# A hybrid attention block: two gates ahead in the merge queue, a first norm that carries its gain, and mask additions and zero fills on VectorE

## The chip, the cores and the metric

The kernel runs on one core of a Trainium2 chip. TensorE (PE) multiplies, VectorE (DVE) and ScalarE (ACT) do element-wise work, GpSimd (POOL) a few additions and subtractions, and the queue of SyncE (SP) issues nearly all DMAs. The metric is device time of the whole program in microseconds (us). A difference is called none when it stays within 1% of the time before.

## The reference

One layer on a sequence of 512 tokens and 1024 model columns, all in float32:

```python
h = _rms(x, norm1_g)                       # x * rsqrt(mean(x*x) + eps) * g
(a_q, a_k, a_v, i_q, i_k, i_w, b_q, b_kv, b_g, c_qkv, mix_g) = _split_last(h @ w_in, IN_SIZES)
y_a = _dsa_attention(...) @ w_branch_a     # 8 heads, keys chosen by an indexer's top 128
y_b = _nsa_attention(...) @ w_branch_b     # 8 heads: compressed, selected-block and window parts
y_c = _dilated_attention(...) @ w_branch_c # 12 heads at strides 1, 4 and 16, mixed by their sums
g = jax.nn.sigmoid(mix_g)                  # 3 x 1024 gate columns
x = x + (g_A * y_a + g_B * y_b + g_C * y_c) @ w_out
h = _rms(x, norm2_g)
gate, up = jnp.split(h @ w_ffn_in, 2, axis=-1)
x = x + (jax.nn.silu(gate) * up) @ w_ffn_out
```

In branch A the selection is an additive mask: the bias table of a head plus, per query and key, zero or a large negative number (`topm`). The softmax adds that sum to the logits.

## The kernel before, in words

**Matrix products.** Every large product is made of three matmuls on halves of the numbers: each operand is a rounded part (`hi`) and a remainder (`lo`), and `mm3` (L106 to L108) adds hi·hi, hi·lo and lo·hi. `weights` (L89 to L102) loads pieces of a weight matrix (`raw`, issued by SP), ScalarE rounds them to `whi` (L81) and VectorE, for some pieces GpSimd, subtracts to `wlo` (L82).

**First norm.** `norm_sums` squares a token tile (128 tokens) in two halves, one on ScalarE (L162), one on VectorE (L164). `norm_T` multiplies by the reciprocal root (halves on VectorE L176 and ScalarE L178), transposes on TensorE into the PSUM pool `tr` of two buffers (L111), multiplies by the gain column `gT` (L188, tile `gx`), and splits into `xh` and `xl`, the latter on GpSimd for one half and VectorE for the other. `gT` is loaded as 1024 single elements.

**Order of the work.** The program is written as a stream of projections and gates, with the attention branches as generators: each `tick` advances every started generator by one step. A scheduler turns this into a fixed order on each engine, so an instruction that is not ready stops all behind it on its engine. DMAs share eight completion lanes: a ninth waits until the lane of the first is free, in the order of issue.

**Gates and merges.** Of each branch (in the order B, A, C) and each of 8 column groups, `gate` (L949) computes the gate with 24 matmuls of 128x512 and two ticks, and `merge` (L965) multiplies the branch's output by its weights (12 matmuls, for C 6) and adds it to the sum in DRAM (`dz`). The list `due` holds gates whose merge is still to come; `ready` ticks the attention on, with nothing between, until the branch's output is there. In the trace a gate matmul reads `pm<-xh` or `pm<-xl`, a merge matmul `pm<-oT`.

**Softmax of a head's query tile** (L538 to L565): logits `lg` on TensorE, table added and maximum on VectorE (L547), exponent on ScalarE (L562), division on VectorE (L563, L564), then transposes of `p`. For branch A with a mask, GpSimd first makes `tabm` = table + `topm` (L557), 24 times.

**Branch C.** `c_load` (L755) brings back projected queries and keys (`c_in`, 12 DMAs, five buffers that it shares with `p`); `c_prep` transposes them one after the other, loads values (`c_v`) and, by 24 small DMAs for two heads, the bias tables (`ctab`, L246). GpSimd zero-fills four buffers `pt12` (L831), of which the last 128 columns of each half are later written whole.

Of the kernel before, what the change touches and what calls it, by code (L numbers as in the profile page):

```python
# [11 lines left out]
F32 = mybir.dt.float32  # L12
# [3 lines left out]
ALU = mybir.AluOpType  # L16
# [51 lines left out]
def block_kernel(ctx: ExitStack, tc: tile.TileContext, x, norm1_g, norm2_g, w_in, qk_norm_g, cmp_pos, cmp_w,  # L68
# [58 lines left out]
    xts = []  # L127
    ipx = ExitStack()
    ip = ipx.enter_context(tc.tile_pool(name="init", bufs=1))
    with tc.high_priority():  # L130
        for t in range(NT):
            xt = ip.tile([128, D], F32, name=f"x{t}")
            nc.sync.dma_start(xt, x[t * 128:(t + 1) * 128, :])
            xts.append(xt)
    gT = ip.tile([128, KC], F32, name="gT")
    nc.scalar.dma_start(gT, norm1_g[0].rearrange("(k p) -> p k", p=128))
    ident = cp.tile([128, 128], F32, name="ident")
    make_identity(nc, ident)
    mhalf = cp.tile([128, 16], F32, name="mhalf")
# [27 lines left out]
    def norm_T(xt, t, ss, n, g, xh, xl, pst, tmp, lo):  # L167

        s1 = ty.tile([128, 16], F32, name="nss", tag="ss")
        nc.vector.tensor_reduce(out=s1[:, 0:1], in_=ss[:, 0:n], op=ALU.add, axis=AX.X)  # L170
        r = rstd(s1, 1, 1.0 / D)
        hn = tmp.tile([128, D], F32, name="hn", tag="hn", bufs=2)
        for q in range(2):
            hs = slice(q * 512, q * 512 + 512)
            if q == 0:
                nc.vector.tensor_scalar(out=hn[:, hs], in0=xt[:, hs], scalar1=r[:, 0:1], scalar2=None, op0=ALU.mult)  # L176
            else:
                nc.scalar.activation(hn[:, hs], xt[:, hs], AF.Copy, scale=r[:, 0:1])  # L178
        yield
        for q in range(2):  # L180
            ps = pst()
            for k in range(4):
                transpose(ps[:, k, :], hn[:, (4 * q + k) * 128:(4 * q + k + 1) * 128])
            ts = slice(t * 128, (t + 1) * 128)
            if g is not None:
                g3 = g[:, 4 * q:4 * q + 4].unsqueeze(2).to_broadcast([128, 4, 128])
                gx = tmp.tile([128, 4, 128], F32, name="gx", tag="gx", bufs=2)
                nc.vector.tensor_tensor(out=gx, in0=ps, in1=g3, op=ALU.mult)  # L188
                ps = gx
            split(xh[:, 4 * q:4 * q + 4, ts], xl[:, 4 * q:4 * q + 4, ts], ps, eng=lo[q])  # L190

    ps1 = ExitStack()
# [13 lines left out]

    xh = xp.tile([128, KC, S], F32R, name="xh", tag="xh")
    xl = xp.tile([128, KC, S], F32R, name="xl", tag="xl")
    for t in range(NT):
        ss = ty.tile([128, 16], F32, name="nss", tag="ss")  # L210
        norm_sums(ss, xts[t], ip)
        for _ in norm_T(xts[t], t, ss, 2, gT, xh, xl, tr_tile, ip, (nc.gpsimd, nc.vector)):
            pass
    nc.sync.dma_start(mk, masks)
    for hh in range(2):
# [33 lines left out]
        return bass.AP(tensor=tab.tensor, offset=tab.offset + hi - 1, ap=[list(tab.ap[0]), [-1, hi - lo]])  # L249


    def proj_tm(segs, evac, then=None):
        width = sum(n for _, n in segs)
        wk = weights(w_in, segs, list(range(KC)), pool=PP)
        for t in range(NT):
            ps = mm_tile()
            ts = slice(t * 128, (t + 1) * 128)
            mm3(ps[:, 0:width], [((xh[:, k, ts], xl[:, k, ts]), wk[k]) for k in range(KC)])
            evac(t, ps)
            tick()  # L260
        if then is not None:
            start(then())
# [19 lines left out]
            yield  # L282

    def tmt(name):
        return ap_.tile([128, NT, 256], F32, name=name, tag="tm", bufs=3)

    def norm_heads(tm, c0, nh):

# [77 lines left out]
    def narrow():  # L366
        aik = scratch4k([128, NT, 256], "aik")

        def evac(t, ps):
            for j, c in enumerate((0, 128)):  # L370
                nc.scalar.copy(undup(aik[:, t, 128 * j:128 * j + 128], 1), dup(ps[:, c:c + 64], 1))
            nc.vector.tensor_copy(av[:, t, :], ps[:, 64:128])
            nc.vector.tensor_copy(iw[:, t, :], ps[:, 192:196])
            nc.scalar.activation(bgt[:, t, :], ps[:, 196:220], AF.Tanh, scale=0.5)  # L374

        def then():
            nc.vector.tensor_scalar(out=bgt, in0=bgt, scalar1=1.0, scalar2=0.5, op0=ALU.add, op1=ALU.mult)
            nc.vector.tensor_scalar(out=bg4[:, 0, :, 0], in0=bg4[:, 0, :, 0], scalar1=live, scalar2=None, op0=ALU.mult)
            norm_heads(aik, 0, 2)
            yield from wait(0)  # L380
            st_["ik"] = k_stack(aik, 128, None)
            yield
            while len(st_.get("iq", ())) < 4:
                yield
            for i in range(1, NT):
                yield from scores(i)
            st_["ak"] = k_stack(aik, 0, gain[:, 1:2])
            yield
            for i in range(1, NT):
                yield from select(i)  # L390

        proj_tm([(C_AKV, 128), (C_IK, 68), (C_BG, 24)], evac, then=then)

    def scores(i):
        w = 128 * (i + 1)
# [154 lines left out]
    def causal_probs(q, i, k, tab, topk, gate):  # L550
        w = 128 * (i + 1)
        lg = lg_tile()
        last_qk[0] = qk(lg[:, 0:w], q, i, k)
        tab = rev(tab, 0, w)
        if topk is not None:
            tm_ = ab.tile([128, S], F32, name="tabm", tag="tabm", bufs=2)
            nc.gpsimd.tensor_tensor(out=tm_[:, 0:w], in0=tab, in1=topk, op=ALU.add)  # L557
            tab = tm_[:, 0:w]
        p = ap_.tile([128, S], F32, name="p", tag="p", bufs=5)
        m = ty.tile([128, 4], F32, name="m", tag="m")  # L560
        add_table(p[:, 0:w], lg[:, 0:w], tab, 3e38, m[:, 0:1])
        nc.scalar.activation(p[:, 0:w], p[:, 0:w], AF.Exp, bias=m[:, 0:1], scale=-1.0, accum_out=m[:, 1:2])  # L562
        nc.vector.reciprocal(m[:, 2:3], m[:, 1:2])  # L563
        nc.vector.tensor_scalar(out=p[:, 0:w], in0=p[:, 0:w], scalar1=m[:, 2:3], scalar2=gate, op0=ALU.mult,  # L564
                                op1=ALU.bypass if gate is None else ALU.mult)  # L565
        return p
# [225 lines left out]
    def c_prep(hf, cz, ld):  # L792
        for g in range(3):
            for s in "qk":
                if hf == 1:
                    c_load()
                    yield
                t_ = c_in.pop((hf, g, s))
                ps = tr_cols(t_, 0)
                if g == 0:  # L800
                    ld[s, g] = (near_queries if s == "q" else near_keys)(hf, cz, ps)
                    if len(c_jobs) > 6:
                        c_load()
                    yield
                    continue
                cq = cz.tile([128, S], F32, name="cq", tag="cq", bufs=8)
                dst = cq
                if s == "q":
                    dst, ps = cq.rearrange("p (i r w) -> p i r w", i=NT, r=4), ps.rearrange("p (i w r) -> p i r w", i=NT, r=4)
                elif g:  # L810
                    dst, ps = cq.rearrange("p (r u) -> p r u", r=4), ps.rearrange("p (u r) -> p r u", r=4)
                nc.scalar.activation(dst, ps, AF.Copy, scale=(gain8[:, 4:5] if s == "q" else gain[:, 5:6]))
                ld[s, g] = cq
                if len(c_jobs) > 6:
                    c_load()
                yield
            rows = dV[g, :, 128 * hf:128 * hf + 128]
            v_ = cz.tile([128, NT, 128], F32, name="c_v", tag="cv", bufs=6)
            nc.sync.dma_start(v_, rows.rearrange("(u r) c -> u r c", r=NT) if g else
                              rows.rearrange("(t p) c -> p t c", p=128))  # L820
            ld["v", g] = v_
        for j in range(2):
            h = 2 * hf + j
            tab = cz.tile([128, S], F32, name="ctab", tag="ctab", bufs=4)
            for r in range(4):
                rows = tab[32 * r:32 * r + 32]
                vec_table(rows[:, 0:256], 16 + h, V_C0 + r, [[4, 32], [1, 256]])
                vec_table(rows[:, 256:384], 20 + h, V_C1, [[1, 32], [1, 128]])
                vec_table(rows[:, 384:512], 24 + h, V_C2, [[1, 32], [1, 128]])
            pt = cz.tile([128, 2, NT, 128], F32, name="pt12", tag="pt12", bufs=3)  # L830
            nc.gpsimd.memset(pt, 0.0)  # L831
            ld["tab", j], ld["pt", j] = tab, pt

    def c_unit(hf, i, j, ld, d):
# [116 lines left out]
    def gate(bi, f):  # L951
# [6 lines left out]
        for k0 in range(0, KC, 4):  # L958
            mm3(pg, [((wg[k][0][:, cs], wg[k][1][:, cs]), (xh[:, k, :], xl[:, k, :])) for k in range(k0, k0 + 4)], k0, KC)
            tick()  # L960
        tz = ap_.tile([128, 2, S], F32, name="tz", tag="tm", bufs=3)
        nc.scalar.activation(tz[:, 0, :], pg, AF.Tanh, scale=0.5)
        return tz

# [62 lines left out]
    for bi in (1, 0, 2):  # L1027
        for f in range(KC):
            due.append((bi, f, gate(bi, f)))
            if len(due) > 1:  # L1030
                if due[0][1] == 0:
                    ready(due[0][0])
                merge(*due.pop(0))
# [137 lines left out]
```

## Time and profile before

| | us |
|---|---|
| median of 3 runs | 993.58 (992.93 to 999.28) |
| the profiled execution, own time | 991.78 |
| its span | 990.0 |
| PE / DVE / ACT / POOL busy | 971.0 / 564.9 / 436.5 / 174.0 |

How to read it: busy time is the sum of an engine's instructions, and matmuls overlap one another a little, so TensorE's 98% does not say that it never waits. The chain of waits follows the last instruction back to what released it, step by step. In a timeline row the idle time in brackets is what the engine waited just before, with the releaser; a row may hold several like instructions.

### The profile page before, as it was taken

The numbers are of one execution on the slowest core, as the hardware profiler recorded it, in microseconds if no ns is written. First come the engines' busy times: TensorE is split into PE (matmuls) and PEld (weight loads), VectorE is DVE, ScalarE is ACT, GpSimd is POOL, SyncE is SP. The second block draws the span as 40 slices with busy tenths as digits, with TensorE's granted clock in tenths as the row PEclk, the third lists the DMA queues.
The fourth block names the chain that finished last, engine by engine and source line by source line (L and its number), as shares of the span: only waits on it lengthen the run. The fifth ranks groups of instructions, "written<-read, shape, count | busy, mean of one in ns | idle before, by whom it ended". The sixth has DMA issues, their size and how long they took to land.

```text
span 990.0 us, 16079 instructions
## 1 busy us (share of the span) xinstructions
PE 971.0 (98%) x5887; PEld 823.7 (83%) x5887; DVE 564.9 (57%) x1277; ACT 436.5 (44%) x956; POOL 174.0 (18%) x156
## 2 busy tenths in 40 slices
PE   6999999999999899999999999999999999999998
PEld 5889999899887577777778899988888888888886
DVE  6699999766665666574764645454344344422321
ACT  5544555756565655564534434443333233322220
POOL 3234565543100221131110312000000000000000
PEclk9999999999999999999999999999999999999999
DMA  8541344433332244367613452233333333322421
GB/s 210 123 128 44 86 119 128 120 116 110 104 96 66 79 129 121 118 167 195 187 57 89 140 201 86 86 101 110 88 88 108 104 85 96 110 93 96 139 75 42
DMA packets 119264, 109.91 MB, mean 111 GB/s; under 512 B 19931, under 2 KB 105234, under 8 KB 119186
## 3 DMA queue, kind: packets, MB, share of 16 engines
q1 hardware_dynamic: 116994, 107.85, 37.6%
q10 hardware_dynamic: 2192, 1.05, 0.4%
q8 instruction: 46, 0.75, 0.3%
q14 instruction: 32, 0.26, 0.1%
HBM read 96.66 MB, written 12.21 MB: 110 GB/s over the span
## 4 chain that ended last, share of the span: by engine, by line
PE 93%; DMA 3%; DVE 2%; ACT 1%; issue 1%; SPq 1%; POOL 0%; DVEq 0%; ACTq 0%; POOLq 0%
PE pf L107 14%; PE pf L108 14%; PE pf L106 14%; PE pm L107 13%; PE pm L106 13%; PE pm L108 13%; PE tr L111 4%; PE ovb L541 2%; PE lg L364 2%; PE lg L363 2%; PE ova L541 1%; DMA c_in<-dC 1%; PE lg L849 1%; DMA raw<-in_w_in 1%; DMA raw<-in_w_branch_a 1%
## 5 line engine op out<-in xcount | busy, mean ns | idle before, releaser
L82 DVE TENSOR_TENSOR wlo<-raw,whi 128x512 fp32r<-128x512 f32 (+1 forms) x243 | 182.4, 756 | 146.1 <-ACT whi L81 145.1
L81 ACT CAST whi<-raw 128x512 fp32r<-128x512 f32 (+1 forms) x288 | 176.9, 619 | 175.0 <-PE pf L108 80.8
L107 PE MATMUL pm<-wlo,xh 128*128 128x256 f32 (+1 forms) x512 | 145.5, 287 | 0.3 <-DVE wlo L82 0.3
L106 PE MATMUL pm<-whi,xh 128*128 128x256 f32 (+1 forms) x512 | 145.1, 288 | 0.6 <-ACT bgt L374 0.6
L108 PE MATMUL pm<-whi,xl 128*128 128x256 f32 (+1 forms) x512 | 144.8, 285 | 0.5 <-POOL xl L82 0.5
L107 PE MATMUL pf<-xl,whi 128*128 128x512 f32 (+1 forms) x384 | 142.6, 372 | 0.1
L106 PE MATMUL pf<-xh,whi 128*128 128x512 f32 (+1 forms) x384 | 142.5, 372 | 0.0
L108 PE MATMUL pf<-xh,wlo 128*128 128x512 f32 (+1 forms) x384 | 142.0, 371 | 0.0
L107 PEld LDWEIGHTS pm<-wlo,xh 128*128 128x128 f32 x512 | 98.1, 192 | 1.9 <-issue 0.8
L108 PEld LDWEIGHTS pm<-whi,xl 128*128 128x128 f32 x512 | 98.2, 192 | 1.4 <-POOL xl L82 0.8
L106 PEld LDWEIGHTS pm<-whi,xh 128*128 128x128 f32 x512 | 97.7, 193 | 1.2 <-ACT bgt L374 0.8
L108 PE MATMUL pm<-xh,wlo 128*128 128x512 f32 x224 | 88.8, 396 | 0.0
L106 PE MATMUL pm<-xh,whi 128*128 128x512 f32 x224 | 88.7, 396 | 0.0
L107 PE MATMUL pm<-xl,whi 128*128 128x512 f32 x224 | 88.1, 393 | 0.0
L107 PEld LDWEIGHTS pf<-xl,whi 128*128 128x128 f32 x384 | 72.3, 188 | 12.5 <-DVE xl L82 0.3
L106 PEld LDWEIGHTS pf<-xh,whi 128*128 128x128 f32 x384 | 72.2, 188 | 12.5
L108 PEld LDWEIGHTS pf<-xh,wlo 128*128 128x128 f32 x384 | 72.2, 188 | 12.6
L82 POOL TENSOR_TENSOR wlo<-raw,whi 128x512 fp32r<-128x512 f32 x45 | 62.2, 1404 | 111.6 <-ACT whi L81 100.8
L106 PE MATMUL pf<-whi,hh 128*128 128x512 f32 x176 | 69.4, 395 | 0.0
L108 PE MATMUL pf<-whi,hl 128*128 128x512 f32 x176 | 69.4, 395 | 0.0
L107 PE MATMUL pf<-wlo,hh 128*128 128x512 f32 x176 | 69.4, 395 | 0.0
L562 ACT ACTIVATE p<-p,m 128x128 f32<-128x128 f32 (+3 forms) x96 | 53.8, 561 | 27.2 <-DVE m L547 26.0
(312 smaller groups left out, 1691.0 us busy)
## 6 DMA issues: line engine op xcount, KB each, us to landing
raw<-in_w_in SPq DMA_DIRECT2D x92, 256.0 KB, 3.1
raw<-in_w_ffn_in SPq DMA_DIRECT2D x88, 256.0 KB, 2.9
raw<-in_w_ffn_out SPq DMA_DIRECT2D x44, 256.0 KB, 2.8
raw<-in_w_in SPq DMA_DIRECT2D x52, 128.0 KB, 2.6
x<-in_x SPq DMA_DIRECT2D x8, 512.0 KB, 6.0
tab<-dvec SPq DMA_DIRECT2D x16, 256.0 KB, 3.3
dz<-tz SPq DMA_DIRECT2D x16, 256.0 KB, 2.5
tz<-dz SPq DMA_DIRECT2D x16, 256.0 KB, 3.3
```

What stands on the lines that cost most here:

```text
L81: nc.scalar.copy(dst_hi, src)
L82: (eng or nc.vector).tensor_tensor(out=dst_lo, in0=src, in1=dst_hi.bitcast(F32), op=ALU.subtract)
L106: nc.tensor.matmul(ps, ah, bh, start=(j == 0), stop=False)
L107: nc.tensor.matmul(ps, ah, bl, start=False, stop=False)
L108: nc.tensor.matmul(ps, al, bh, start=False, stop=(j == n - 1))
L111: nc.tensor.transpose(dst, src, ident[0:src.shape[0], 0:src.shape[0]])
L363: nc.tensor.matmul(lg, qs, k[:, 0, 0:w], start=True, stop=False)
L364: return nc.tensor.matmul(lg, qs, k[:, 1, 0:w], start=False, stop=stop)
L541: mm = nc.tensor.matmul(ov[64 * j:64 * j + 64, 128 * b:S], v(b), pts[j][:, 4 * b:3 * b + NT, :], start=first and b == 0, stop=last and b = ...
L562: nc.scalar.activation(p[:, 0:w], p[:, 0:w], AF.Exp, bias=m[:, 0:1], scale=-1.0, accum_out=m[:, 1:2])
L849: nc.tensor.matmul(lg[32 * r:32 * r + 32, c:c + n], ld["q", g][hp, 128 * i + 32 * r:128 * i + 32 * r + 32], ld["k", g][hp, 128 * r:128 * r ...
```

## The change

The gain row `g_row` (one DMA of 1024 contiguous elements) is spread over the partitions by two matmuls with a row of ones, into two PSUM tiles. `norm_T` multiplies by root and gain in one VectorE instruction, before the transposes; the multiplication after them is gone, `xh` and `xl` are made from the transposes' PSUM tile, and VectorE makes all of `xl`. Squares are taken by ScalarE alone. The first weights are loaded from an earlier place in the text (SP's order of the first loads comes out as before). VectorE makes `tabm`, in the buffers `work`, and zero-fills `pt12` without the columns that are written later. `due` holds one gate more, with a fourth buffer.

```diff
+    NARROW = [(C_AKV, 128), (C_IK, 68), (C_BG, 24)]
+    g_row = ip.tile([1, D], F32, name="g_row")
+    nc.scalar.dma_start(g_row, norm1_g[0:1, :])
+    one = ip.tile([1, 128], F32, name="one")
+    nc.vector.memset(one, 1.0)
...
-    gT = ip.tile([128, KC], F32, name="gT")
-    nc.scalar.dma_start(gT, norm1_g[0].rearrange("(k p) -> p k", p=128))
+            if t == 1:
+                w_narrow = weights(w_in, NARROW, list(range(KC)))
...
-        nc.vector.tensor_reduce(out=s1[:, 0:1], in_=ss[:, 0:n], op=ALU.add, axis=AX.X)
-        r = rstd(s1, 1, 1.0 / D)
+        if n > 1:
+            nc.vector.tensor_reduce(out=s1[:, 0:1], in_=ss[:, 0:n], op=ALU.add, axis=AX.X)
+        r = rstd(s1 if n > 1 else ss, 1, 1.0 / D)
...
-            if q == 0:
+            if g is not None:
+                nc.vector.scalar_tensor_tensor(out=hn[:, hs], in0=xt[:, hs], scalar=r[:, 0:1], in1=g[q], op0=ALU.mult,
+                                               op1=ALU.mult)
+            elif q == 0:
...
-            if g is not None:
-                g3 = g[:, 4 * q:4 * q + 4].unsqueeze(2).to_broadcast([128, 4, 128])
-                gx = tmp.tile([128, 4, 128], F32, name="gx", tag="gx", bufs=2)
-                nc.vector.tensor_tensor(out=gx, in0=ps, in1=g3, op=ALU.mult)
-                ps = gx
...
+    gps = [lg_tile() for _ in range(2)]
+    for q in range(2):
+        nc.tensor.matmul(gps[q], one, g_row[:, 512 * q:512 * q + 512], start=True, stop=True)
...
-        norm_sums(ss, xts[t], ip)
-        for _ in norm_T(xts[t], t, ss, 2, gT, xh, xl, tr_tile, ip, (nc.gpsimd, nc.vector)):
+        norm_sums(ss, xts[t], ip, n=1)
+        for _ in norm_T(xts[t], t, ss, 1, gps, xh, xl, tr_tile, ip, (nc.vector, nc.vector)):
...
-        return ap_.tile([128, NT, 256], F32, name=name, tag="tm", bufs=3)
+        return ap_.tile([128, NT, 256], F32, name=name, tag="tm", bufs=4)
...
-            tm_ = ab.tile([128, S], F32, name="tabm", tag="tabm", bufs=2)
-            nc.gpsimd.tensor_tensor(out=tm_[:, 0:w], in0=tab, in1=topk, op=ALU.add)
+            tm_ = ab.tile([128, S], F32, name="tabm", tag="work", bufs=3)
+            nc.vector.tensor_tensor(out=tm_[:, 0:w], in0=tab, in1=topk, op=ALU.add)
...
-            nc.gpsimd.memset(pt, 0.0)
+            nc.vector.memset(pt[:, :, 0:NT - 1, :], 0.0)
...
-        tz = ap_.tile([128, 2, S], F32, name="tz", tag="tm", bufs=3)
+        tz = ap_.tile([128, 2, S], F32, name="tz", tag="tm", bufs=4)
...
-            if len(due) > 1:
+            if len(due) > 2:
```

The first place is VectorE's order where branch B has ended and branch A's softmaxes begin again. Before:

```order
L564 TENSOR_SCALAR p<-p,m 128x256
L582 TENSOR_TENSOR oT<-ovb,oT 128x512
L563 RECIPROCAL m<-m 128x1
L547 ISA p,m<-lg,tabm 128x512
L547 ISA m 128x1
L563 RECIPROCAL m<-m 128x1
L564 TENSOR_SCALAR p<-p,m 128x384
```

In the change:

```order
L589 TENSOR_TENSOR oT<-ovb,oT 128x512
L571 TENSOR_SCALAR p<-p,m 128x256
L564 TENSOR_TENSOR tabm<-tab,topm_1580 128x256
L571 TENSOR_SCALAR p<-p,m 128x384
L564 TENSOR_TENSOR tabm<-tab,topm_1580 128x256
L554 ISA p,m<-lg,tabm 128x512
```

Two additions of 256 columns now stand among the divisions that the transposes wait for; one of 384 and two of 512 stand up to 16 rows ahead of them.

The second place is SP's order where branch C's inputs are loaded, from the first `c_in` to the tables. Before:

```order
L93 DMA raw<-in_w_branch_a 128x2x256 x2
L761 DMA c_in<-dC 128x4x128 x2
L93 DMA raw<-in_w_in 128x2x256
L761 DMA c_in<-dC 128x4x128 x2
L93 DMA raw<-in_w_in 128x2x256
L761 DMA c_in<-dC 128x4x128 x2
L819 DMA c_v<-dV 128x4x128 x3
L246 DMA ctab<-dvec 32x256
```

In the change:

```order
L93 DMA raw<-in_w_branch_a 128x2x256
L93 DMA raw<-in_w_in 128x2x256 x4
L768 DMA c_in<-dC 128x4x128 x6
L826 DMA c_v<-dV 128x4x128 x3
L253 DMA ctab<-dvec 32x256
```

Behind these stand, in both, the rest of the 24 `ctab` DMAs and only then the seventh `c_in`. One store of `dz` stands among the tables in both, one `raw` before and two in the change.

The third place is TensorE's order at the sixth and seventh of the `c_in` transposes. Before:

```order
L106 MATMUL pm<-xh,whi 128x512
L107 MATMUL pm<-xl,whi 128x512
L108 MATMUL pm<-xh,wlo 128x512
L111 MATMUL tr<-ident,c_in 128x128 x4
L849 MATMUL lg<-cq 32x32 x8
L106 MATMUL pm<-xh,whi 128x512
L107 MATMUL pm<-xl,whi 128x512
L108 MATMUL pm<-xh,wlo 128x512
L106 MATMUL pm<-xh,whi 128x512
L107 MATMUL pm<-xl,whi 128x512
L111 MATMUL tr<-ident,c_in 128x128 x4
```

In the change:

```order
L106 MATMUL pm<-oT,whi 128x512
L107 MATMUL pm<-oT,whi 128x512
L111 MATMUL tr<-ident,c_in 128x128 x4
L856 MATMUL lg<-cq 32x32 x4
L111 MATMUL tr<-ident,c_in 128x128 x4
L856 MATMUL lg<-cq 32x32 x4
L108 MATMUL pm<-oT,wlo 128x512
```

The seventh transposes have moved up: from the first `c_in` transposes to the seventh there were 32 gate and 30 merge matmuls, and now there are 24 and 20, while the rest between them stays but for four small `lg<-cq`.

## Rows read from the trace of the kernel before

**Rows 1.** The page: busy time per engine; the chain's shares by engine
```profile
PE 971.0 (98%) x5887; PEld 823.7 (83%) x5887; DVE 564.9 (57%) x1277; ACT 436.5 (44%) x956; POOL 174.0 (18%) x156
PE 93%; DMA 3%; DVE 2%; ACT 1%; issue 1%; SPq 1%; POOL 0%; DVEq 0%; ACTq 0%; POOLq 0%
```

**Rows 2.** Windows: length, busy and instructions of PE, PEld, DVE, ACT, POOL, clock, DMA
```profile
350.00:430.00 80.00, 80.00 (x415) 63.74 (x415) 48.85 (x127) 43.48 (x106) 19.32 (x19) 1.00 0.37 109
540.00:990.00 450.00, 446.24 (x2242) 379.29 (x2240) 186.45 (x293) 143.15 (x257) 22.33 (x26) 1.00 0.34 103
```

**Rows 3.** SP's waits from 0 to 30 us: total, times, longest
```profile
SPq L93 <- DMA gT<-in_norm_g: 1.3, 1, 1.3
```

**Rows 4.** PE's timeline, start: start, length, instruction, idle before and releaser
```profile
13.07 0.55 PE L108 MATMUL pm<-whi,xl 128*128 128x220 f32 x1 [0.49 <-POOL xl L82]
18.14 0.53 PE L107 MATMUL pm<-wlo,xh 128*128 128x220 f32 x1
18.67 0.27 PE L106 MATMUL pm<-whi,xh 128*128 128x220 f32 x1
```

**Rows 5.** Groups from 0 to 35 us: busy, mean ns, idle before
```profile
L82 POOL TENSOR_TENSOR xl<-gx,xh 128x512 fp32r<-128x512 f32 x4 | 5.4, 1356 | 6.7 <-ACT xh L81 6.6
L188 DVE TENSOR_TENSOR gx<-tr,gT 128x512 f32<-128x512 f32 x8 | 5.4, 683 | 0.1
L82 DVE TENSOR_TENSOR xl<-gx,xh 128x512 fp32r<-128x512 f32 x4 | 3.7, 922 | 1.7 <-ACT xh L81 1.7
```

**Rows 6.** Line 238, a float32 matmul with few rows: shortest, median, longest ns
```profile
L238 PE MATMUL lg<-oh,rel x6: 536/546/557, 49.6 to 68.5; 33*28 33x448 f32 x6
```

**Rows 7.** PE's timeline where only the attention runs
```profile
328.56 0.55 PE L111 MATMUL tr<-ident,p 128*128 128x128 f32 x3 [0.73 <-ACT pT L530]
330.02 0.66 PE L111 MATMUL tr<-ident,p 128*128 128x128 f32 x4 [0.42 <-ACT pT L530]
331.36 0.65 PE L111 MATMUL tr<-ident,p 128*128 128x128 f32 x4 [0.68 <-DVE qst L321]
332.71 4.02 PE L541 MATMUL ovb<-pT,bv 128*64 128x512 f32 x16 [0.52 <-ACT pT L530]
```

**Rows 8.** DVE's groups from 320 to 435 us
```profile
L564 DVE TENSOR_SCALAR p<-p,m 128x256 f32<-128x256 f32 x8 | 5.6, 705 | 0.2
L547 DVE CUSTOM_DVE_ANT_0 p<-lg,tabm 128x512 f32<-128x512 f32 x8 | 5.5, 684 | 4.0 <-PE lg L364 4.0
L547 DVE CUSTOM_DVE_ANT_0 p<-lg,tabm 128x384 f32<-128x384 f32 x8 | 4.4, 552 | 2.2 <-PE lg L364 2.1
L547 DVE CUSTOM_DVE_ANT_0 p<-lg,tabm 128x256 f32<-128x256 f32 x8 | 3.4, 423 | 8.3 <-PE lg L364 8.3
L564 DVE TENSOR_SCALAR p<-p,m,bgt 128x256 f32<-128x256 f32 x2 | 0.8, 410 | 0.0
```

**Rows 9.** DVE's timeline at the end of branch A
```profile
432.00 0.48 DVE L564 TENSOR_SCALAR p<-p,m 128x512 f32<-128x512 f32 x1
437.76 0.69 DVE L582 TENSOR_TENSOR oT<-ova,oT 128x512 fp32r<-128x512 f32 x1 [4.61 <-ACT oT L581]
```

**Rows 10.** PE's timeline, from branch A's last logits to branch C's preparation
```profile
429.22 0.39 PE L363 MATMUL lg<-kst,qst 128*128 128x512 f32 x1
434.16 0.63 PE L111 MATMUL tr<-ident,c_in 128*128 128x128 f32 x4
434.72 2.38 PE L541 MATMUL ova<-pT,av 128*64 128x512 f32 x16
443.44 0.40 PE L108 MATMUL pm<-xh,wlo 128*128 128x512 f32 x1
446.64 0.40 PE L107 MATMUL pm<-xl,whi 128*128 128x512 f32 x1
456.61 0.63 PE L111 MATMUL tr<-ident,c_in 128*128 128x128 f32 x4 [0.95 <-DMA c_in<-dC]
```

**Rows 11.** SP's timeline there: start and length of the DMA issues
```profile
434.07 1.89 SPq L761 DMA_DIRECT2D c_in<-dC  x2
436.01 2.97 SPq L819 DMA_DIRECT2D c_v<-dV  x3
445.44 6.96 SPq L246 DMA_DIRECT2D ctab<-dvec  x15
452.50 0.52 SPq L761 DMA_DIRECT2D c_in<-dC  x1
```

**Rows 12.** The DMAs of `c_in`, issue to landing: shortest, median, longest us
```profile
DMA to landing us min/median/max: 3.5/4.0/4.3
```

**Rows 13.** The chain of waits at the eighth `c_in`: start, length, what
```profile
462.86 3.66 DMA c_in<-dC
```

More of the change, by code (lines that the diff above doesn't have):

```diff
@@ L249, in rev, with proj_tm @@
         return bass.AP(tensor=tab.tensor, offset=tab.offset + hi - 1, ap=[list(tab.ap[0]), [-1, hi - lo]])
-    def proj_tm(segs, evac, then=None):
+    def proj_tm(segs, evac, then=None, wk=None):
         width = sum(n for _, n in segs)
-        wk = weights(w_in, segs, list(range(KC)), pool=PP)
+        wk = wk or weights(w_in, segs, list(range(KC)), pool=PP)
         for t in range(NT):
@@ L390, in then @@
                 yield from select(i)
-        proj_tm([(C_AKV, 128), (C_IK, 68), (C_BG, 24)], evac, then=then)
+        proj_tm(NARROW, evac, then=then, wk=w_narrow)
     def scores(i):
```

## The prediction

> **What bounds the kernel now.** I read the page first. TensorE is busy for 971.0 of 990 us and carries 93% of the chain of waits, VectorE is busy 57% and GpSimd 18% [rows 1]. Taking work from GpSimd is therefore worth nothing by itself, and nothing in the change takes away a matmul of the large products. A gain can come only from places where TensorE waits, so I read the windows next. From 540 to 990 us TensorE is at 446.24 of 450, and from 350 to 430 at 80.00 of 80 [rows 2]. What is left are four places: the start, 327 to 346 us (attention with no gates between), the end of branch A (429 to 441), and branch C's preparation (434 to 467). For these I read the timelines of TensorE, VectorE and SP, and asked at each what the new order puts there.
>
> **The start.** The load of `gT` holds a completion lane, and SP's ninth DMA waits 1.3 us for it [rows 3]; one contiguous row should land sooner, so the loads behind it can come at most about 1.3 us earlier. VectorE loses eight `gx` multiplications (5.4 us) and four half squares; it gains four `xl` that GpSimd made (4 x 0.92 = 3.7) and four more `hn` [rows 5], so it comes out about even. GpSimd's 1.36 us for an `xl` leaves the path, and with it a wait of 0.49 at 13.07 [rows 4, 5]. Against this, `xl` is now the last reader of a transpose's PSUM tile, of which there are two, so the next transposes wait for it; and the two gain matmuls stand ahead of all others. Their nearest row is a float32 matmul of 448 columns, 0.55 us [rows 6]: 2 x 0.55 x 512/448 = 1.25 us, and twice that, 2.5, while the engine runs at its lower clock, as the narrow projection does until 18.67 (its matmuls fall from 0.53 to 0.27 long, [rows 4]). Most of that lies ahead of the first normed tile, where TensorE has nothing else. Bounds: +2 if they and the PSUM tiles hold the first transposes up, -3 if the loads gain 1.3 and an engine that works earlier also reaches the higher clock earlier. I take **-1.0**, next to the one wait that is measured, 1.3.
>
> **327 to 346 us.** `ready` for branch B is reached one gate later, so 16 of a gate's matmuls now stand between the transposes of its last softmaxes. They would fill some of the idle time there, but behind them two long rows of transposes, the `aq_in` transposes and the sums `ovb` still follow each other as before, with the four waits (0.73 + 0.42 + 0.68 + 0.52 = 2.35 us), after which the 16 `ovb` matmuls took 4.02 us [rows 7] where a like group took 2.38 [rows 10]: the engine had fallen to its lower level. I give the gate 0.8 us, between 0 and 2.35 + (4.02 - 2.38) = 4.0. Then branch A restarts, and there VectorE is the one that is waited for. Five additions that GpSimd made stand in or just ahead of that stretch: two of 256, one of 384, two of 512 columns. VectorE's own row of the same widths, two inputs and one output, gives 0.423, 0.552 and 0.684 [rows 8], together 2.77 us. Something comes back: a division of 128x256 took 0.705 on the mean in this stretch, and 0.410 for the two in branch B, where GpSimd did not add [rows 8]. Four of them give 4 x 0.295 = 1.2. So 0 to +1.6, and I take +1.0, since part of the additions falls into waits for logits. Both together **+0.2**.
>
> The Trainium skill, page "SBUF — State Buffer", section "Who interferes with whom", says why: VectorE and GpSimd share a pair of SBUF ports, and a VectorE instruction in a two-port mode and a GpSimd instruction exclude each other. By that rule every stretched division here becomes short again. It would take all eight, 8 x 0.295 = 2.4 us, from VectorE, and turn my +1.0 into about -0.2 were they all waited for; the trace bears the stretching out with 0.705 against 0.410, but not that all eight are waited for.
>
> Of the other 19 additions three stand earlier, among branch B's softmaxes, and the rest falls between 350 and 430 us, where TensorE never stops and VectorE is busy for 48.85 of 80 us [rows 2]. These are hidden by the gates that stand between logits and transposes; all 24 are 8 x 0.423 + 8 x 0.552 + 8 x 0.684 = 13.3 us, so VectorE stays below 80%. Were that cover gone, each would cost its 0.4 to 0.7 us.
>
> **The zero fills.** Three of four stand right behind the last division of branch A and ahead of the subtraction `oT<-ova`, ahead of which VectorE was idle for 4.61 us [rows 9]. A fill of 2 x 384 columns is bounded by two VectorE rows of 384, 1.1 us [rows 8]; three are at most 3.3. They cost nothing, and if that idle time were gone, up to 3.3.
>
> **The end of branch A.** Before, the last logits (429.22) were followed by eight gate matmuls before TensorE came to transposes of `p`; the last division ended at 432.48 [rows 9, 10]. In the new order no gate matmul is left behind the last logits: transposes, two merge matmuls, and transposes follow. A gate matmul starts every 3.20/14 = 0.229 us [rows 10], so 8 x 0.229 = 1.8 us of cover go. Some of it comes back from what else stands there: **+1.3**, of 0 to 1.8.
>
> **Branch C's inputs.** This is the largest term. The sixth `c_in` needs the buffer of the first, so it is issued only after the first `c_in` transposes (434.16); then SP issues three `c_v`, 24 `ctab` (0.46 us each, 6.96/15) and a store and a load, and the seventh `c_in` only at 452.50 [rows 10, 11]. It lands 4.0 us later [rows 12]: 456.5, which is 22.3 us after the first transposes. TensorE came to it 21.5 us after them, and waited 0.95 [rows 10]. In the new order SP's row is the same but for one load more, while TensorE has 32 - 24 = 8 gate and 30 - 20 = 10 merge matmuls less in between: 18 x 0.229 = 4.1 us less work. The wait grows from 0.95 to 5.1: **+4.1** (0 if SP gets through its row that much sooner, +6 if the further load waits too). The matmuls are not saved, they stand elsewhere, where TensorE was already full. The eighth `c_in` is on the chain too [rows 13]. Ahead of it SP has 20 rows instead of 14, some 6 x 0.46 = 2.8 us, and TensorE five merge matmuls more, 1.1: up to +1.6, and 0 if loads among those rows wait less than before; I take **+1.0**.
>
> **The clock.** Idle time of 2.35 us in pieces was followed by the lower level, which cost 4.02 - 2.38 = 1.6 us; a single wait of 0.95 was not. A wait of 5 us lies beyond both, but little work stands right behind it: half, **+0.8**, of 0 to 1.6.
>
> **Sum.** -1.0 + 0.2 + 1.3 + 4.1 + 1.0 + 0.8 = +6.4. Against the profiled execution's own 991.78 that is 998.2. The median of the runs is 993.58, 1.8 above it, and the result will be such a median: **1000.0**.
>
> **The rivals.**
> *No new wait* (0.20). SP is ahead of TensorE in the new order, or the store and loads among the tables wait less, so that the seventh `c_in` lands in time. For it: SP's issues follow one another with small waits. Against: the sixth `c_in` can't be issued before the first is transposed, which ties SP to TensorE. Then 993.6 - 1.0 + 0.2 + 1.3 = 994.
> *Gaps filled* (0.10). The start gains its 3, and the extra gate closes the waits of 327 to 333 and the clock doesn't fall (-4.0), without a new wait in branch C: 993.6 - 3 - 4.0 = 986.6. Against: the rows at 328.56 to 332.71 stand as before.
> *SP blocked* (0.15). One of the two `raw` loads among the tables needs a buffer freed by merges that TensorE has behind its own wait; the seventh `c_in` comes later by a full load and rounding. Price: another landing of 4.0 plus the clock's other half 0.8, 1000.0 + 4.8 = 1004.8, slower than before by over 1%. It decides from the point where SP waits for VectorE's `wlo` ahead of the seventh `c_in`. In the trace of before SP's row there shows no such wait.
> The forecast has 0.55.
>
> **Range and chances.** The range runs from just above the filled gaps, 988, to the forecast with the bounds of its unknown terms and with SP blocked: 1006. About 1% is what a measurement of this kernel can tell from no change, so the borders are 983.6 and 1003.5. Faster: a third of the filled gaps and a little else, 0.05. Slower: most of the blocked case and a seventh of the forecast, 0.18. Within: 0.77.
>
> **What would show it.** In the profile after: the first seven transposes of `c_in` with a wait of about 5 us ahead of the seventh, released by its DMA, and SP's issue of it about 18 us after the first transposes; a lower clock or longer matmuls just behind; the first narrow matmul about 1 us earlier; the divisions near 0.41 at 256 columns; TensorE full from 350 to 430. I am wrong if no wait of over 2 us stands at the seventh `c_in`, if the waits of 327 to 333 are gone, or if VectorE's additions show as releasers of TensorE between 350 and 430.

## The result, and the profile after

| | before | changed |
|---|---|---|
| median, us | 993.62 (14 runs, 991.28 to 999.28) | 1000.94 (14 runs, 998.53 to 1002.5) |
| ratio of runs, 95% interval | 1 | 1.0069 [1.0055, 1.0083] |
| span of the profiled execution, us | 990.0 | 998.8 |
| PE / DVE / POOL busy, us | 971.0 / 564.9 / 174.0 | 976.8 / 566.7 / 140.8 |

The change is slower by 0.7%, some 7 us in the medians and 8.8 between the two profiled executions. By the measure of 1% that is no difference, though the interval leaves out 1. The forecast was 1000.0. VectorE is hardly busier than before: what was added to it, and what went, cancel. GpSimd lost 33 us of work, and the kernel is not faster for it.

**The start** became shorter: the sixteen `ovb` matmuls that began at 229.27 us before begin at 228.70. TensorE's timeline (start, length, instruction, idle before it and releaser):

```profile
3.23 3.75 PE L215 MATMUL lg<-g_row,one 1*128 1x512 f32 x4 [3.23 <-DMA g_row<-in_norm_g]
7.33 1.12 PE L111 MATMUL tr<-ident,hn 128*128 128x128 f32 x4 [0.35 <-DVE hn L182]
10.96 1.12 PE L111 MATMUL tr<-ident,hn 128*128 128x128 f32 x4 [2.52 <-DVE hn L182]
14.91 0.61 PE L107 MATMUL pm<-wlo,xh 128*128 128x220 f32 x2
15.34 0.30 PE L108 MATMUL pm<-whi,xl 128*128 128x220 f32 x1
```

The gain matmuls cost 3.75 us, more than my upper 2.5, but in time that TensorE has free. The narrow matmuls drop to about 0.3 at 15.34, where they did at 18.67 [rows 4], and SP no longer waits for the load of the gain, as it did [rows 3].

**327 to 354 us.** VectorE's timeline, then TensorE's:

```profile
335.56 0.89 DVE L564 TENSOR_TENSOR tabm<-tab,topm 128x256 f32<-128x256 f32 x2 [1.56 <-DMA tab<-dvec]
336.56 0.55 DVE L571 TENSOR_SCALAR p<-p,m,bgt 128x512 f32<-128x512 f32 x1
```

```profile
333.64 0.66 PE L111 MATMUL tr<-ident,aq_in 128*128 128x128 f32 x4 [0.53 <-ACT pT L537]
334.72 0.66 PE L111 MATMUL tr<-ident,p 128*128 128x128 f32 x4 [0.42 <-ACT pT L537]
337.25 1.09 PE L111 MATMUL tr<-ident,p 128*128 128x128 f32 x4 [1.88 <-DVE p L571]
339.26 4.23 PE L548 MATMUL ovb<-pT,bv 128*64 128x512 f32 x16 [0.60 <-ACT pT L537]
346.53 0.44 PE L370 MATMUL lg<-kst,qst 128*128 128x384 f32 x1 [0.38 <-DVE m L554]
348.29 0.74 PE L106 MATMUL pm<-oT,whi 128*128 128x512 f32 x2 [0.44 <-ACT oT L588]
350.55 0.50 PE L107 MATMUL pm<-oT,whi 128*128 128x512 f32 x1 [0.55 <-DVE oT L589]
353.13 0.50 PE L106 MATMUL pm<-oT,whi 128*128 128x512 f32 x1 [0.86 <-DVE tz L986]
```

Two additions wait 1.56 us for a table's load, and behind them on VectorE stands the last division of branch B. On GpSimd no division stood behind such an addition. So TensorE waits 1.88 us for that division, in the place where it waited 0.68 for `qst` [rows 7]; the others of those rows are there as before (0.53, 0.42, 0.60), and so is the lower clock in `ovb` (4.23 against 4.02), which now begins sooner, at the transposes ahead of it (1.09 against 0.65). The extra gate filled next to nothing. The four waits of the restart sum to 2.23 us; before there was one, 0.71.

**The end of branch A.** VectorE, then TensorE:

```profile
434.97 0.42 DVE L554 CUSTOM_DVE_ANT_0 p<-lg,tabm 128x256 f32<-128x256 f32 x1 [4.13 <-PE lg L371]
435.44 0.69 DVE L564 TENSOR_TENSOR tabm<-tab,topm 128x512 f32<-128x512 f32 x1
436.64 0.69 DVE L564 TENSOR_TENSOR tabm<-tab,topm 128x512 f32<-128x512 f32 x1
440.47 0.42 DVE L571 TENSOR_SCALAR p<-p,m 128x384 f32<-128x384 f32 x1
442.94 2.31 DVE L838 MEMSET pt<- 128x768 f32 x3
447.70 0.69 DVE L589 TENSOR_TENSOR oT<-ova,oT 128x512 fp32r<-128x512 f32 x1 [2.45 <-ACT oT L588]
```

```profile
441.04 0.52 PE L111 MATMUL tr<-ident,p 128*128 128x128 f32 x3 [1.42 <-ACT p L569]
449.47 0.32 PE L851 MATMUL lg<-cks,cqs 128*128 128x128 f32 x1
451.00 0.33 PE L851 MATMUL lg<-cks,cqs 128*128 128x128 f32 x1 [1.21 <-DVE cks L794]
451.73 0.49 PE L106 MATMUL pm<-oT,whi 128*128 128x512 f32 x1 [0.39 <-DVE tz L986]
453.14 0.63 PE L107 MATMUL pm<-oT,whi 128*128 128x512 f32 x1
453.56 0.63 PE L108 MATMUL pm<-oT,wlo 128*128 128x512 f32 x1
463.67 0.60 PE L111 MATMUL tr<-ident,c_in 128*128 128x128 f32 x4
465.20 0.63 PE L111 MATMUL tr<-ident,c_in 128*128 128x128 f32 x4 [0.73 <-DMA c_in<-dC]
478.15 0.66 PE L111 MATMUL tr<-ident,c_in 128*128 128x128 f32 x4 [1.60 <-DMA c_in<-dC]
482.08 0.63 PE L108 MATMUL pm<-oT,wlo 128*128 128x512 f32 x1
```

VectorE is busy from 435 to 442.9 but for 0.30 us, with two additions of 0.69 in that chain, and TensorE waits 1.42 for a softmax [rows 9 show the old chain's end]. The three fills take 2.31 and are followed by an idle time of 2.45, as forecast. But then comes a wait that I had not seen: 1.21 us for the second keys `cks` of branch C and 0.39 more, and behind it eight merge matmuls, of which the last six start 0.43 us apart instead of 0.23. The seventh `c_in` (465.20) waits 0.73 us, no more than before [rows 10]; the eighth, 1.60. The windows give the granted clock (the third number from the end; 1.00 is the upper level, 2.4 GHz, and 0.50 the lower):

```profile
440.00:450.00 10.00, 8.42 (x48) 5.32 (x48) 6.69 (x15) 6.53 (x14) 0.00 (x0) 1.00 0.77 224
450.00:460.00 10.00, 8.61 (x35) 6.98 (x36) 6.29 (x10) 4.49 (x8) 2.95 (x2) 0.83 0.41 109
470.00:480.00 10.00, 8.40 (x83) 6.44 (x81) 3.74 (x17) 2.83 (x7) 1.63 (x1) 0.98 0.70 191
480.00:490.00 10.00, 10.00 (x79) 7.60 (x72) 7.86 (x23) 5.55 (x13) 0.76 (x1) 0.85 0.59 178
```

It is at the upper level until the wait for the keys and until the one of 1.60 us, and partly at the lower one behind each of them. At the restart it is below 1.00 as well, 0.81 from 330 to 340 and 0.85 from 340 to 350, where before it was 0.83 and 1.00. From 540 us on the two profiles lose the same within 2 us.

### The profile page after: what moved, and what is told of

The parts are those of the page before. It is cut to its first block, busy times and chain, and to the rows that moved or that the text cites. A ratio compares the mean times of both kernels' runs of the same rounds, so it can differ in the third digit from the quotient of the medians.

```text
span 998.8 us, 16011 instructions
## 1 busy us (share of the span) xinstructions
PE 976.8 (98%) x5891; PEld 825.9 (83%) x5891; DVE 566.7 (57%) x1294; ACT 435.8 (44%) x952; POOL 140.8 (14%) x124
## 4 chain that ended last, share of the span: by engine, by line
PE 93%; DVE 2%; DMA 2%; ACT 1%; issue 1%; SPq 0%; POOL 0%; DVEq 0%
PE pf L108 14%; PE pf L107 14%; PE pf L106 14%; PE pm L106 13%; PE pm L107 13%; PE pm L108 13%; PE tr L111 5%; PE ovb L548 2%; PE lg L371 2%; PE lg L370 2%; PE ova L548 1%; PE lg L856 1%; DMA x<-in_x 1%; PE ovc L901 1%; DMA c_v<-dV 1%
## 5 line engine op out<-in xcount | busy, mean ns | idle before, releaser
L82 DVE TENSOR_TENSOR wlo<-raw,whi 128x512 fp32r<-128x512 f32 (+1 forms) x243 | 177.4, 735 | 144.3 <-ACT whi L81 143.9
```

The lines of the kernel that those rows point to most:

```text
L82: (eng or nc.vector).tensor_tensor(out=dst_lo, in0=src, in1=dst_hi.bitcast(F32), op=ALU.subtract)
```

## The experiments

Each version was timed along with the kernel before, and its ratio is to those executions, so versions are compared by the ratio and not by the bare time. In the expectations, theory S says that SP's row of loads ahead of branch C's seventh input sets the time, theory V that VectorE's own new work costs, and theory Q that the longer queue costs by itself.

**The four parts.** The norm alone:

```diff
-        norm_sums(ss, xts[t], ip)
-        for _ in norm_T(xts[t], t, ss, 2, gT, xh, xl, tr_tile, ip, (nc.gpsimd, nc.vector)):
+        norm_sums(ss, xts[t], ip, n=1)
+        for _ in norm_T(xts[t], t, ss, 1, gps, xh, xl, tr_tile, ip, (nc.vector, nc.vector)):
...
```

with the lines of the change that go with it.

> The kernel before with the new first norm alone. By the two traces the lost time up to 40 us is 1.0 us less in the changed kernel: 992.6 us, within 992 to 993.2. A rival, that the two gain matmuls and the transposes that wait for the split eat it up: 993.6 to 995 us.

992.66 us, ratio 0.9993 [0.9975, 1.0011]: as expected, though the interval holds no gain as well.

The queue alone:

```diff
-            if len(due) > 1:
+            if len(due) > 2:
...
-            tm_ = ab.tile([128, S], F32, name="tabm", tag="tabm", bufs=2)
+            tm_ = ab.tile([128, S], F32, name="tabm", tag="work", bufs=3)
```

> The kernel before with two gates ahead and four buffers alone; the masks' additions stay on GpSimd but take their tile from the buffers of another tag, since four buffers don't fit otherwise. Its order has 52 gate and 30 merge matmuls from the first to the seventh transposes of branch C's inputs. Theory S: no loss in branch C, some filled idle time at the end of branch B: 992 to 994 us. A third theory Q (a longer queue costs by itself, since the work it moves is missing at the end of branch A): 996 to 1000 us. Theory V: 993.6 us.

991.95, 0.9982 [0.9971, 0.9993]: a small gain. Theory Q falls, and it is not the longer queue alone that takes the work out from between branch C's transposes: it puts 52 gate matmuls there, not 24. This version has the shared buffers too, so they are not what costs either.

The changed kernel without the queue:

```diff
-            if len(due) > 2:
+            if len(due) > 1:
...
```

with three buffers again.

> The changed kernel with the merge queue back at one gate ahead (and three buffers); all else as changed. Its fixed order has 36 gate and 30 merge matmuls from the first transposes of branch C's inputs to the seventh (before 32 and 30, changed kernel 24 and 20). Theory S (the load row of SP ahead of the seventh input sets the time, and TensorE with too little work in between loses it): no loss there, about 993.6 - 1.0 (start) + up to 2.5 (additions at branch A's restart) = 993 to 995 us. Rival V (VectorE's own new work, additions and fills, is what costs): nearly all of the loss stays, 999 to 1001 us.

1006.58, 1.0131 [1.0115, 1.0148], worse than either theory gave, although 36 and 30 matmuls stand between the transposes. The queue takes back a good part of what the rest costs.

The changed kernel without the additions:

```diff
-            nc.vector.tensor_tensor(out=tm_[:, 0:w], in0=tab, in1=topk, op=ALU.add)
+            nc.gpsimd.tensor_tensor(out=tm_[:, 0:w], in0=tab, in1=topk, op=ALU.add)
```

> The changed kernel with the 24 additions of the masks back on GpSimd; queue, norm and fills as changed. Its order has 36 gate and 30 merge matmuls from the first to the seventh transposes. Theory S: no loss in branch C, 992 to 994 us. Theory V: the additions are most of the loss, so also 992 to 994 us, and the wait of VectorE for a table's load at 335 us is gone. Theory Q: 997 to 1000 us.

994.3, 1.0004 [0.9993, 1.0016]: the additions are the largest part. In its trace TensorE waits 0.68 us again at the last transposes of branch B, and at the end of branch A the wait of 1.42 is gone. Alone, on the kernel before, the edit the other way round (and the shared buffers):

> The kernel before with the masks' additions alone on VectorE (in the shared buffers). TensorE's order is that of before from the first transposes of branch C's inputs to the ninth. Theory T (the additions cost only where they stand, at branch B's end and branch A's restart, by a table's load that VectorE waits for and by the divisions behind them): 995 to 997 us, and branch C loses what it lost before. Rival V (the additions cost what separates the changed kernel from the same with the additions on GpSimd, 1000.9 - 994.3 = 6.6): 999 to 1001 us.

999.83, 1.0058 [1.0037, 1.008]: rival V. Theory T underrated the place at the end of branch A. There VectorE's and GpSimd's timelines of this kernel show a division and the zero fills of GpSimd side by side, and TensorE's what waited:

```profile
436.00 2.35 DVE L564 TENSOR_SCALAR p<-p,m 128x384 f32<-128x384 f32 x1
```

```profile
435.39 2.74 POOL L831 MEMSET pt<- 128x1024 f32 x3 [174.22 <-DVE m L547]
```

```profile
332.66 0.63 PE L111 MATMUL tr<-ident,p 128*128 128x128 f32 x4 [1.75 <-DVE p L564]
438.49 0.87 PE L111 MATMUL tr<-ident,p 128*128 128x128 f32 x3 [2.01 <-DVE p L564]
```

The division took 2.35 us where others of its size take 0.42 in the changed kernel; the wait of 1.75 is the table's load again. The Trainium skill's rule of the shared ports ("SBUF — State Buffer", "Who interferes with whom") has GpSimd and a two-port VectorE instruction shut each other out, and says that the one issued later waits for the whole of the other. The trace agrees, and goes further: the division waited through most of three fills in a row.

Norm and fills, without additions and queue:

```diff
-            nc.gpsimd.memset(pt, 0.0)
+            nc.vector.memset(pt[:, :, 0:NT - 1, :], 0.0)
```

> The kernel before with the new first norm and the zero fills on VectorE; additions on GpSimd, one gate ahead. Its order has 24 gate and 20 merge matmuls between the first and the seventh transposes of branch C's inputs, as in the changed kernel, where the new norm alone had 32 and 30. Theory S (that order loses time behind SP's row, whatever moved it): 996 to 998 us, with TensorE waiting some 5 us in all between the first transposes and the eighth. Rival (the order does not matter, the fills are hidden): 992 to 993 us, as the norm alone.

997.64, 1.003 [1.0012, 1.0048], against 0.9993 for the norm alone. The time lies in theory S's range, and TensorE's waits from the first transposes to the eighth sum to the 5 us that it gave (1.21 + 0.39 + 1.37 + 2.31 = 5.28). The order has 24 and 20 matmuls there with one gate ahead, so it is the fills that bring it, not the queue. The same edit on queue and norm takes 0.9967 to 1.0004. So the fills cost 0.37% both times, though they never stand in TensorE's way themselves. And the changed kernel with the fills back:

> The changed kernel with the zero fills back on GpSimd. Its order has 52 gate and 30 merge matmuls between the first and the seventh transposes of branch C's inputs, where the changed kernel has 24 and 20. Theory F (the fills on VectorE cost 0.37% by the order that they bring about in branch C, as the norm with and without them, and queue and norm with and without them, differ): 996.5 to 998 us. Rival (the fills are hidden, and the order is the queue's): 1000 to 1001.5 us. A division of VectorE beside a fill of GpSimd may take over 2 us, as with the additions alone.

998.79, 1.0056 [1.0039, 1.0074]: 0.13% less than with them, which is less than theory F gave and within the noise of the two. With the fills back on GpSimd, the collision of the additions alone returns (a division of 1.91 us at 439.88, and TensorE waits 2.90):

```profile
441.93 0.88 PE L111 MATMUL tr<-ident,p 128*128 128x128 f32 x3 [2.90 <-DVE m L570]
```

The two parts that gained, which is the changed kernel with the other two undone:

```diff
-            nc.vector.tensor_tensor(out=tm_[:, 0:w], in0=tab, in1=topk, op=ALU.add)
+            nc.gpsimd.tensor_tensor(out=tm_[:, 0:w], in0=tab, in1=topk, op=ALU.add)
...
-            nc.vector.memset(pt[:, :, 0:NT - 1, :], 0.0)
+            nc.gpsimd.memset(pt, 0.0)
```

> The two parts that gained, together: two gates ahead and the new norm; additions and fills on GpSimd. 52 gate and 30 merge matmuls stand between the first and the seventh transposes. If the parts add up: 993.7 - 1.8 - 1.1 = 990.8 us. Rival (the norm's shift of the work spoils the queue's order): 993 us or more.

991.02, 0.9967 [0.9954, 0.998]: they add up, and beat both kernels, by less than the 1%. The clock stays at the upper level in all ten-microsecond windows from 430 to 480, as here:

```profile
440.00:450.00 10.00, 9.51 (x48) 6.00 (x46) 6.22 (x9) 6.07 (x11) 2.58 (x2) 1.00 0.70 202
450.00:460.00 10.00, 10.00 (x56) 8.16 (x55) 6.30 (x10) 5.52 (x9) 1.51 (x2) 1.00 0.50 135
```

| parts | ratio | 95% interval |
|---|---|---|
| norm | 0.9993 | 0.9975 to 1.0011 |
| queue | 0.9982 | 0.9971 to 0.9993 |
| queue, norm | 0.9967 | 0.9954 to 0.9980 |
| norm, fills | 1.0030 | 1.0012 to 1.0048 |
| queue, norm, fills | 1.0004 | 0.9993 to 1.0016 |
| additions | 1.0058 | 1.0037 to 1.0080 |
| queue, norm, additions | 1.0056 | 1.0039 to 1.0074 |
| norm, additions, fills | 1.0131 | 1.0115 to 1.0148 |
| all four | 1.0069 | 1.0055 to 1.0083 |

**What the fills do.** In every version with the fills on VectorE (the changed kernel and six of the experiments) the wait of 1.21 us for `cks` is there, and in every version with them on GpSimd (before and six) it is not. The orders show why. Before, and in all versions without the fills, 8 or 12 merge matmuls stand between the two first `lg<-cks`; with them there is none, the two are a pair, and the merges come behind:

```
L107 MATMUL pm<-oT,whi 128x512
L108 MATMUL pm<-oT,wlo 128x512
L851 MATMUL lg<-cks,cqs 128x128 x2
L106 MATMUL pm<-oT,whi 128x512
```

The second keys take VectorE two instructions (1.50 us for both), and TensorE stands. The scheduler's fixed order was turned by 2.3 us of VectorE time that, on the chip, fell into idle time.

What follows such a wait is not always the same. In the version with queue, norm and fills the same two waits stand there and the clock stays up: it is 1.00 from 440 to 460, and the merges behind them start 0.23 us apart. In the norm alone TensorE waits 2.08 us for an input, and the clock is 1.00 from 450 to 470. Two rows of the first version and one of the second:

```profile
446.36 0.33 PE L851 MATMUL lg<-cks,cqs 128*128 128x128 f32 x1 [1.21 <-DVE cks L794]
448.13 0.40 PE L107 MATMUL pm<-oT,whi 128*128 128x512 f32 x1
456.95 0.63 PE L111 MATMUL tr<-ident,c_in 128*128 128x128 f32 x4 [2.08 <-DMA c_in<-dC]
```

Nor is it the same in every execution of one kernel. Of norm and fills' twelve, with one fixed order, the one with a mean granted clock of 1.000 took 993.0 us and the three at 0.991 took 999.8 on the mean. Of the 87 executions of the kernel before beside the experiments, 32 at 1.000 took 992.3, and four at 0.995 some 997. So a large part of the fills' 0.37% goes with the clock, and in the one execution at 1.000 little of it is left. The changed kernel's fourteen have 0.994 on the mean, those 87 have 0.998. At the 0.8 to 1 us for each 0.001 that these figures give, 3 to 4 of its 7 us would go with the clock; that is an estimate, and among the fourteen themselves the time hardly follows it.

**Is SP's load row the limit?** The prediction's largest term rested on that.

```diff
-                vec_table(rows[:, 256:384], 20 + h, V_C1, [[1, 32], [1, 128]])
-                vec_table(rows[:, 384:512], 24 + h, V_C2, [[1, 32], [1, 128]])
+                vec_table(rows[:, 256:512].rearrange("p (g c) -> p g c", g=2), 20 + h, V_C1,
+                          [[1, 32], [4 * VEC + V_C2 - V_C1, 2], [1, 128]])
```

> The changed kernel with branch C's tables loaded by 16 DMAs for 24 (two pieces of a head's table in one, the same bytes). TensorE's order is that of the changed kernel up to the ninth of branch C's inputs. SP's row ahead of the seventh input is shorter by 8 x 0.46 = 3.7 us. Theory S: the waits at the seventh (0.73) and the eighth (1.60) input and the lower clock behind the latter go, 997 to 998 us; the wait for the second keys at 451 us stays. Rival (the seventh and eighth are late for another reason): 1000.5 to 1001.5 us.

1003.48, 1.0094 [1.0072, 1.0117], slower than either theory gave. The seventh `c_in` was issued 4.1 us sooner, counted from the first transposes, and came in time. But the second half's tables moved up ahead of the eighth, which was issued when it was in the changed kernel (474.31 against 474.62) and took 5.87 us to land instead of 3.49:

```profile
480.23 1.11 PE L111 MATMUL tr<-ident,c_in 128*128 128x128 f32 x4 [5.15 <-DMA c_in<-dC]
```

So shortening SP's row in front only moved the wait. The other test takes the inputs out of that row:

```diff
-            nc.sync.dma_start(t_, dC[n, :, :, c0:c0 + 128])
+            nc.scalar.dma_start(t_, dC[n, :, :, c0:c0 + 128])
```

> The changed kernel with branch C's twelve input loads issued from ScalarE's queue instead of SP's, so that they don't stand behind the tables. The fixed order there has 36 gate and 30 merge matmuls between the first and the seventh transposes. Theory S: no wait of TensorE for an input's load of over 0.5 us is left, 996 to 998 us; the wait for the second keys may stay. Rival (the waits turn up elsewhere, at keys, or at work of ScalarE that now stands behind a load's wait): 999 to 1002 us.

1001.22, 1.0089 [1.0066, 1.0112]: one wait for a load is left, 1.08 us, but there is no gain. The wait for the keys and the lower clock behind it stay, and so do those at the restart; the order of the matmuls is another one too (36 and 30 between the first and seventh transposes):

```profile
452.75 0.33 PE L851 MATMUL lg<-cks,cqs 128*128 128x128 f32 x1 [1.21 <-DVE cks L794]
478.72 0.66 PE L111 MATMUL tr<-ident,c_in 128*128 128x128 f32 x4 [1.08 <-DMA c_in<-dC]
```

Theory S, that this row by itself sets the time of the changed kernel, falls. The same edit on queue and norm:

> Two gates ahead and the new norm, additions and fills on GpSimd, and branch C's input loads from ScalarE's queue: a try at a version that beats both kernels. The queue and norm together gave 0.9967 of before; that version's loss in branch C is already near that of before, so 0 to 1.5 us more: 0.995 to 0.997. Rival (ScalarE held up by the loads' waits): 0.998 to 1.002.

989.88, 0.997 [0.9956, 0.9983]: no different from 0.9967, so that version loses nothing that this edit could win.

**Where do the additions cost?**

```diff
-            nc.vector.tensor_tensor(out=tm_[:, 0:w], in0=tab, in1=topk, op=ALU.add)
+            (nc.vector if 0 < pair[0] < 3 else nc.gpsimd).tensor_tensor(out=tm_[:, 0:w], in0=tab, in1=topk, op=ALU.add)
...
```

> The changed kernel with 12 of the 24 additions, those of branch A's second and third pair of heads, on VectorE, and those of the first and the last pair (where branch A restarts and where it ends) on GpSimd. With all on GpSimd the ratio to before was 1.0004, with all on VectorE 1.0069. Theory E (the additions cost only at the two ends, where TensorE has no gates between logits and transposes and VectorE is waited for; in the middle they are hidden): 1.000 to 1.002. Rival (each addition costs about as much, wherever it stands): half of the difference stays, 1.003 to 1.005.

997.64, 1.0036 [1.002, 1.0052]: by the total, the rival. By the trace, half of it is theory E: the wait at the last division of branch B is back at 0.68, as before.

```profile
336.18 0.66 PE L111 MATMUL tr<-ident,p 128*128 128x128 f32 x4 [0.68 <-DVE qst L328]
438.75 0.52 PE L111 MATMUL tr<-ident,p 128*128 128x128 f32 x3 [0.73 <-DVE p L571]
449.44 0.33 PE L853 MATMUL lg<-cks,cqs 128*128 128x128 f32 x1 [1.21 <-DVE cks L796]
476.44 0.66 PE L111 MATMUL tr<-ident,c_in 128*128 128x128 f32 x4 [1.82 <-DMA c_in<-dC]
```

In place of the rest there are waits of 0.49 and 0.73 us at the end of branch A, where the order is another one again, with no gate left to cover GpSimd's slower additions, and in branch C the eighth input's 1.82, with the lower clock behind it and behind the keys. Here too the time goes with the clock: two executions at 0.998 took 993.7 us, three at 0.993 took 999.1 on the mean. So the cost at the restart is shown, and that the middle additions are free is not: no version changed them alone.

## Why the prediction was right, and where it was not

The time was right, 1000.0 against 1000.94, and so was the sign. The breakdown was right in part only, and by the prediction's own sign its account was wrong: no wait of over 2 us stands at the seventh `c_in`. In the table the measured column adds up TensorE's waits of the two profiles at each place, except for the start.

| term | forecast | measured | from |
|---|---|---|---|
| start | -1.0 | -0.7 to -1.5 | norm alone; queue with and without the norm |
| 327 to 354 us | +0.2 | +3.2 | waits 3.43 - 2.35, then 2.23 - 0.71; lower clock, `ovb` 4.23 - 4.02 and transposes 1.09 - 0.65 |
| end of branch A | +1.3 | +1.4 | the wait at 441.04 |
| seventh `c_in` | +4.1 | -0.2 | 0.73 - 0.95 |
| second keys | none | +1.4 | 1.21 + 0.39, less 0.16 before |
| eighth `c_in` | +1.0 | +1.6 | 1.60 |
| lower clock in branch C | +0.8 | +3 | eleven matmuls at 0.43 for 0.23, and smaller ones, behind both waits |

With -1.0 for the start the measured ones sum to some +9; the spans differ by 8.8. Three steps failed, and that their errors cancelled, so that the time came out within a microsecond, was luck.

*The seventh `c_in`.* "TensorE has 8 gate and 10 merge matmuls less in between: 4.1 us less work" was true of the order, and the load did land some 21 us after the first transposes (443.82), not far from the 22.3 worked out. But I subtracted work from before's elapsed time as if nothing else could fill it. The wait for the keys, 1.6 us, and the lower clock behind it (six matmuls, 0.2 us each, and transposes that took 0.4 more) took some 3 of those 4 us: TensorE came to the seventh input 20.7 us after the first (465.20 - 0.73 - 443.82), where before it had come after 21.5. Where a load's time is fixed, waits ahead of it come out of its slack; had the keys been in time, most of their wait should have stood at the load instead. That fits the two tests that took a wait for a load away and gained nothing, but it is argued: in both, other waits moved too, and no version had the keys in time with all else the same.

*The restart.* "Five additions, 2.77 us, less 1.2 that comes back" priced the additions by their length. The relief was larger than I took: a division of 256 columns now takes 0.350 us on the mean against 0.705 [rows 8].

```profile
L571 DVE TENSOR_SCALAR p<-p,m 128x256 f32<-128x256 f32 x8 | 2.8, 350 | 0.1
L564 DVE TENSOR_TENSOR tabm<-tab,topm 128x256 f32<-128x256 f32 x7 | 2.9, 417 | 1.6 <-DMA tab<-dvec 1.6
```

The prices of the additions were right too (0.417 against 0.423). What was missing from the sum is what the second row has at its end, a wait of 1.6 us for a load, which on GpSimd held up no division and on VectorE held up branch B's last. The trace of before had a hint that I did not use: GpSimd's `tabm` waited for tables' loads.

*The fills.* "They cost nothing" was right for the instructions, three in 2.31 us ahead of idle time, and wrong for the kernel: 0.37% by the order that came with them. The order was in front of me, and the prediction doesn't ask which part brings it; norm and fills, without queue and additions, have the same 24 and 20. The second keys have no term in the sum at all, and the clock's +0.8 was given for one wait, where it fell behind two and longer at the restart. The Trainium skill's rule on the shared ports would have made the restart cheaper; the stretching went as it says, and the wait for the load outweighed it.

What came as written: SP's issue of the seventh input 17.7 us after the first transposes (461.48 against "about 18"), short divisions, no cost of the fills where they stand, and 1.4 at the end of branch A. The first narrow matmul came 0.1 us earlier, not 1 (11.73 against 11.84). Of the rival *no new wait* the seventh input came true, by waits ahead of it that the rival did not have, and the time, 994, did not. *Gaps filled* did not come, since the waits of 327 to 333 were not closed. *SP blocked* did not come either, though the joined tables show what it would look like, 5.15 us at an input. One reading was loose: the DMA that waited for `gT` [rows 3] was the ninth of all and SP's eighth.

## What to carry to other kernels

An instruction moved to another engine takes its waits along: ask what it waits for, and what then stands behind it, before pricing its length. In a kernel with a fixed order per engine, separate the parts of a change and compare their orders, since a part that is free by itself can turn the order elsewhere. Waits that follow one another on one path share their slack: their sizes don't add up, and removing one may give nothing. Look at the granted clock of each execution beside its time: an order that loses little at the upper level can lose much when the clock falls behind its waits.

## What the runs showed of the hardware

Three float32 fills on GpSimd, one right behind the other, held a single VectorE division for 2.35 us instead of 0.42. TensorE's clock was at the lower level for some 3 us behind a wait of 1.21 + 0.39 us at 449.8 to 451.7 and behind one of 1.60. Single waits of 0.95 [rows 10] left it alone, but so did 1.21 + 0.39 in queue, norm and fills, and 2.08 in the norm alone: the length of the wait did not settle it, and what did is not shown. Two matmuls of 512 columns with one row of float32 took 3.75 us at the start, in four recorded pieces, three times the 1.25 that a row of 448 columns at the upper clock [rows 6] gives for two.
